# First 256 tokens of a decoder layer turned and multiplied without their norm, the norm's roots applied to five results

## The chip, the cores and the metric

The kernel runs on one core of one Trainium2 chip. The metric is device time in microseconds (us). Each instruction belongs to an engine: PE multiplies matrices, DVE and ACT do elementwise work on tiles, POOL (GpSimd) does a little of that and issues some transfers, and SP issues most transfers. Each engine runs its own instructions in the order in which it gets them.

## The reference

One layer is computed for 512 prompt tokens and 32 sample tokens (8 sequences of 4), with a model width of 1024. What matters here is its beginning:

```python
def _rmsnorm(x, g):
    x32 = x.astype(jnp.float32)
    y = x32 * lax.rsqrt(jnp.mean(x32 * x32, axis=-1, keepdims=True) + EPS) * g.astype(jnp.float32)
    return y.astype(x.dtype)
...
h = _rmsnorm(x, norm_mix_pre)
proj = h @ w_in
xr, q, k, v, g = jnp.split(proj, [c0, c1, c2, c3], axis=-1)
```

The root (the reciprocal root of a token's mean square) is one number for each token, and the gain `g` is one number for each of the 1024 inputs. Behind this stand a convolution and a recurrent unit on `xr`, windowed attention on `q`, `k` and `v`, gates, an output projection, a second norm, a feed-forward part with a convolution, and the states that are handed on.

## The kernel before

Activations are kept turned: model inputs on the 128 partitions, tokens along the free axis. The tokens are cut into two halves (line 26, `HALF`): the first has 256 columns, the second 288 (256 prompt tokens and the 32 sample tokens). The input projection is worked in blocks of 128 output columns. One **result** is one such block for one half: eight input chunks `k`, and for each chunk three multiplications, since every operand is held as a high and a low part: weights high by `hH`, weights high by `hL`, weights low by `hH` (`mmhalf`, lines 313 to 320). So a result is 24 matrix multiplications into one PSUM buffer.

Weights arrive raw (`wload`, line 244; one block is 512 KB), and are split by half blocks called units: ACT writes the high part (`wsplit_hi`, line 264), DVE the low part (`wsplit_lo`, line 279; POOL does it for the first block).

The order of PE, ACT, DVE and POOL is the order in which the program writes their instructions (`manual_schedule`). `step` (line 322) writes one result and then calls `tick` (line 192). A tick writes, in this order: the high splits of weights that are due, the side work that is due (`sides`: generators such as `norm_b`, the attention's units, the parameters), what the last result left in `late` (usually its `done`, which takes the result out of PSUM and splits it), the low splits, and what was put into `last`. Three PSUM buffers hold results (`psm`, line 132), so result n+3 cannot start before the `done` of result n is over. Five more (`psx`) hold turned tiles and small products.

The five first blocks (`FIRST`, line 72; one of k, one of v, three of q) are multiplied for the first half of the tokens, then the same five for the second half; after that both halves of a block follow each other. I number them: results 1 to 5, results 6 to 10, and from 11 on the pairs.

The beginning is written out by hand, lines 341 to 473. The loads go to SP in this order: `x0`, gains, `x1`, weight blocks 0 and 1, `x2`, `x3`, `x4` (the sample tokens), block 2, small tables, blocks 3 and 4. Each `x` tile holds 128 tokens and is loaded as two column halves of 256 KB. PE meanwhile multiplies constants (`dummy`, line 377: `WARM` 12 times, then the turning of the gains, then `KEEP` 11 times). `xsquares` (line 402) sums squares, one half on ACT and one on DVE; `xrstd` and `newton_rstd` (lines 410 and 387) make the roots, with a square root on ACT between steps on DVE. For `x0` and `x1` the four half tiles are multiplied by their roots (`scale0`, line 440), turned on PE (line 460), and multiplied by the gains and split by `hsplit` (line 429: ACT the high part, DVE the low part). Result 1 (`first_mm`, line 449) is interleaved with this by hand.

The second half of the tokens is normed beside results 2 to 5 by `norm_b` (line 495): squares and roots in tick 1, scaling in tick 2, turning in two groups of four chunks in ticks 3 and 4. `keep_a` and `keep_b` (lines 482 and 485) copy the turned and normed tokens to `xn`; `put_away` (line 488) sends them and the reciprocal of the roots to DRAM, so that `x` can be had again for the residual.

Of the kernel before, what the change touches and what calls it, by code (L numbers as in the profile page):

```python
# [17 lines left out]
P = 128  # L18
# [103 lines left out]
def hawk_step(ctx, tc, I, O):  # L122
# [198 lines left out]

    def step(key, X, a, done, target=None, look=2, quick=False):
# [27 lines left out]
    def xload(i):  # L350
        t0, n, src = TOK[i]
        for z in range(2):
# [12 lines left out]
    relx = cp.tile([NBK, NH], F32, name="relx")  # L365
    nc.sync.dma_start(out=relx, in_=I["rel_bias"])
# [4 lines left out]
    wload(3)  # L371
    wload(4)
    pv = keep.tile([P, 96], F32, name="pv")
# [26 lines left out]
    dve.memset(ss, 1.0)  # L400

    def xsquares(i):
        n = TOK[i][1]
        jk, jv = T(f"jk{i}"), T(f"jv{i}")
        act.activation(jk[:n, 0:512], xt[i, 0][:n, 0:512], AF.Square, accum_out=ss[:n, 0, i:i + 1])
        xb = xt[i, 1][:n, 0:512]
        dve.scalar_tensor_tensor(out=jv[:n, 0:512], in0=xb, scalar=1.0, in1=xb, op0=ALU.mult, op1=ALU.mult,
                                 accum_out=ss[:n, 1, i:i + 1])

# [23 lines left out]

    xsquares(0)
    xsquares(1)
    act.copy(pv[:, 0:8], ps0[:, 0:8])
    xrstd(0, 2)
    u0, u1 = wclaim(2)

    def scale0(i, z):  # L440
        dve.tensor_scalar(xt[i, z][:, 0:512], xt[i, z][:, 0:512], ss[:, 1, i:i + 1], None, ALU.mult)
# [10 lines left out]
    ps_ta = []  # L452
    wsplit_lo(*wsplit_hi(u0), eng=pool)
    seq = (0, 2, 1, 3, 4, 6, 5, 7)
    for z, k in enumerate(seq + (None,) * 3):
        if z % 4 == 0 and z < KD:
            for kk in (z // 2, z // 2 + 1):
                ps_ta.append(PX(f"ps_ta{kk}"))
                for q in range(4):
                    pe.transpose(ps_ta[-1][:, q * P:(q + 1) * P], xtile(q % 2, 2 * kk + q // 2), ident)  # L460
        if k is not None:
            hsplit(k, 0, ps_ta[k // 2][:, k % 2 * 256:k % 2 * 256 + 256])
        if z == 1:
            wsplit_lo(*wsplit_hi(u1), eng=pool)
        if z == 2:
            dummy(0)
            dummy(1)
        if 2 <= z < KD + 2:
            first_mm(seq[z - 2], 0, 0, start=z == 2)
        if z >= 3:  # L470
            first_mm(seq[z - 3], 0, 1)
    for k in range(KD):
# [14 lines left out]

    def put_away():
        dve.reciprocal(rms, ss[:, 1, :])
# [5 lines left out]
    def norm_b():  # L495
        last.extend(lambda i=i: xsquares(i) for i in (2, 3, 4))
        last.append(lambda: xrstd(2, 5))
        yield
        last.extend(lambda i=i, e=e: xscale(i, e) for i, e in ((2, "av"), (3, "av"), (4, "vv")))
        last.extend(lambda k=k: keep_a(k) for k in range(4))  # L500
        yield
        for k in range(4, KD):
            keep_a(k)
        for k in range(KD):
            ps = PX(f"ps_tb{k}")
            for i in (2, 3, 4):
                t0, n, _ = TOK[i]
                pe.transpose(ps[:, t0 - 256:t0 - 256 + n], xtile(i, k), ident[:n, :n])
            late.append(lambda k=k, ps=ps: hsplit(k, 1, ps[:, :288]))
            tb.append(ps)  # L510
            if k % 4 == 3:
                late.extend(lambda k=k, ps=tb[k]: keep_b(k, ps) for k in range(k - 3, k + 1))
            if k in (3,):
                yield


    rows_b = cp.tile([64, P], F32, name="rows_b")
# [130 lines left out]

    def split_ps(X, k, a, ps, extra=()):
        n = HALF[a][1] - HALF[a][0]  # L650
        act.activation(X.get(k, a, 0), ps[:, :n], AF.Copy)
        for dst, src in extra:
            act.copy(dst, src)
        sub(X.get(k, a, 1), ps[:, :n], f32(X.get(k, a, 0)))

    def q_done(hd, a, ps):
        if a == 0:
            Q.alloc(hd)
            split_ps(Q, hd, a, ps)
        else:  # L660
            split_ps(Q, hd, a, ps, [(qs[:, :, hd, :], ps[:, 256:288].rearrange("p (b t) -> p b t", b=DB))])
# [10 lines left out]
    def k_done(kv, a, ps):  # L672
        if a == 0:
            K.alloc(kv)
            split_ps(K, kv, a, ps)
        else:
# [19 lines left out]
    def v_done(kv, a, ps):  # L696
# [3 lines left out]
        v = vtmp[kv]  # L700
        act.activation(v[:, lo:hi], ps[:, :hi - lo], AF.Copy)
        if a == 1:
# [1206 lines left out]
```

## Time and profile before

| | |
|---|---|
| median of 3 runs | 997.24 us (997.2 to 997.45) |
| profiled execution, its own time | 998.22 us |
| span of its instructions | 995.9 us, 20166 instructions |
| PE busy | 986.5 us (99%), 7811 instructions |
| DVE busy | 731.6 us (73%) |
| ACT busy | 579.7 us (58%) |
| POOL busy | 167.2 us (17%) |
| moved by DMA | 135.90 MB |

Times inside the trace count from the first instruction of the span; 2.3 us of the profiled execution lie outside it. A timeline row reads: start, length, engine, line, operation, the tiles written and read, the number of instructions merged, and in brackets how long the engine stood idle before and for whom it waited. A matrix multiplication's length includes its passage through the array, so that neighbours overlap: what a stream of them costs is the distance of their starts. "PEld" rows are weight loads beside PE. `SPq` rows are transfers being issued.

### The profile page before, as it was taken

The page shows a single profiled execution, that of the slowest core. Times are in us where ns is not written, and L with a number is a line of the kernel's source. Part 1 is how long each engine was busy: PE and PEld are TensorE (multiplying, and loading weights), DVE is VectorE, ACT ScalarE, POOL GpSimd, SP SyncE. Part 2 cuts the span into 40 slices and gives each one's busy share as a digit, 9 for nine tenths or more (in the row PEclk, how much of TensorE's full clock was granted, in tenths as well). Part 3 has the DMA queues.
Part 4 walks back from the last instruction along what each step waited for, and adds up shares of the span by engine and source line. Part 5 has one row for each costly group of instructions (what it writes and reads, how often), then busy time and mean ns, then how long its engine had stood idle before and what let it go on. Part 6 is the DMA issues. An engine that isn't in the chain of part 4 may idle for free.

```text
span 995.9 us, 20166 instructions
## 1 busy us (share of the span) xinstructions
PE 986.5 (99%) x7811; PEld 976.2 (98%) x7811; DVE 731.6 (73%) x1537; ACT 579.7 (58%) x1417; POOL 167.2 (17%) x277
## 2 busy tenths in 40 slices
PE   9999999999999999999999999999999999999997
PEld 8999999999999999999999999999999999999996
DVE  6477687645936656589787788888888888888765
ACT  6535455469458625456776655555655555556652
POOL 1152010002304473210001010101010101011004
PEclk9999999999999999999999999999999999999999
DMA  7756323333322634236147767676767676768612
GB/s 209 184 142 216 90 71 104 103 86 102 91 84 86 207 92 140 74 106 196 47 117 155 164 151 168 151 167 152 166 152 167 152 167 152 167 145 205 196 45 90
DMA packets 211782, 135.90 MB, mean 136 GB/s; under 512 B 9501, under 2 KB 197677, under 8 KB 211656
## 3 DMA queue, kind: packets, MB, share of 16 engines
q1 hardware_dynamic: 199720, 113.00, 39.8%
q0 software_dynamic: 11920, 19.59, 12.1%
q10 hardware_dynamic: 48, 2.03, 0.8%
q8 instruction: 61, 1.00, 0.4%
q14 instruction: 33, 0.27, 0.1%
HBM read 112.06 MB, written 11.37 MB: 124 GB/s over the span
## 4 chain that ended last, share of the span: by engine, by line
PE 94%; DVE 2%; DMA 1%; ACT 1%; SPq 1%; issue 0%; DVEq 0%; ACTq 0%
PE pmin L163 21%; PE pmdn L163 17%; PE pux L1458 16%; PE puy L1458 8%; PE pq L1458 6%; PE pmout L163 5%; PE pmlo L163 5%; PE pmao L163 5%; PE puz L1458 4%; PE pg L163 1%; PE psc L163 1%; PE pvp L163 1%; PE ptok L163 1%; SPq L354 1%; DMA raw_in<-in_w_in_dram 1%; PE pt L753 1%
## 5 line engine op out<-in xcount | busy, mean ns | idle before, releaser
L163 PE MATMUL pmin<-hH,wh_in 128*128 128x256 f32 (+1 forms) x568 | 165.9, 292 | 0.0
L163 PE MATMUL pmin<-hL,wh_in 128*128 128x256 f32 (+1 forms) x568 | 163.6, 288 | 0.0
L163 PE MATMUL pmin<-hH,wl_in 128*128 128x256 f32 (+1 forms) x568 | 163.3, 287 | 0.3 <-DVE wl_in L280 0.3
L163 PE MATMUL pmdn<-fH,wh_dn 128*128 128x256 f32 (+1 forms) x448 | 129.3, 289 | 0.1
L163 PE MATMUL pmdn<-fH,wl_dn 128*128 128x256 f32 (+1 forms) x448 | 129.2, 288 | 0.0
L163 PE MATMUL pmdn<-fL,wh_dn 128*128 128x256 f32 (+1 forms) x448 | 129.0, 288 | 0.0
L175 DVE SCALAR_TENSOR_TENSOR uc<-u,fv,uc 128x560 f32<-128x560 f32 x128 | 102.0, 797 | 13.3 <-ACT uc L1489 13.2
L163 PEld LDWEIGHTS pmin<-hH,wh_in 128*128 128x128 f32 x568 | 107.0, 188 | 1.5 <-issue 1.2
L163 PEld LDWEIGHTS pmin<-hH,wl_in 128*128 128x128 f32 x568 | 106.8, 188 | 0.5 <-DVE wl_in L280 0.5
L163 PEld LDWEIGHTS pmin<-hL,wh_in 128*128 128x128 f32 x568 | 107.0, 188 | 0.0
L163 PEld LDWEIGHTS pmdn<-fH,wh_dn 128*128 128x128 f32 x448 | 84.4, 188 | 0.5 <-issue 0.5
L163 PEld LDWEIGHTS pmdn<-fL,wh_dn 128*128 128x128 f32 x448 | 84.3, 188 | 0.0
L163 PEld LDWEIGHTS pmdn<-fH,wl_dn 128*128 128x128 f32 x448 | 84.3, 188 | 0.0
L1584 ACT COPY u<-pux 128x272 f32<-128x272 f32 x52 | 20.1, 387 | 84.2 <-PE pux L1458 84.1
L166 DVE TENSOR_TENSOR u<-puy,u 128x240 f32<-128x240 f32 (+2 forms) x78 | 24.6, 344 | 49.5 <-PE puy L1458 32.3
L172 DVE TENSOR_TENSOR ft<-ft,pmdn 128x256 f32<-128x256 f32 (+1 forms) x104 | 45.2, 435 | 17.1 <-PE pmdn L163 16.5
L275 ACT ACTIVATE wh_in<-raw_in 128x512 fp32r<-128x512 f32 x72 | 44.4, 631 | 17.0 <-PE pmin L163 5.8
L1489 ACT ACTIVATE uc<-u,fv 128x560 f32<-128x560 f32 x64 | 48.2, 755 | 0.0
L280 DVE TENSOR_TENSOR wl_in<-raw_in,wh_in 128x512 fp32r<-128x512 f32 x70 | 46.9, 683 | 0.8 <-ACT wh_in L275 0.7
L716 ACT ACTIVATE s<-s,st 128x256 f32<-128x256 f32 (+1 forms) x32 | 15.2, 475 | 50.6 <-DVE st L713 41.4
L1384 POOL DMA_DIRECT2D raw_up_s<-raw_up_s x26 | 22.7, 874 | 99.9 <-DMA raw_up_s<-raw_up__10515 4.5
L166 DVE TENSOR_TENSOR wl_dn<-raw_dn,wh_dn 128x512 fp32r<-128x512 f32 x56 | 38.3, 684 | 0.0
(781 smaller groups left out, 3426.6 us busy)
## 6 DMA issues: line engine op xcount, KB each, us to landing
raw_in<-in_w_in_dram SPq DMA_DIRECT2D x36, 512.0 KB
raw_dn<-in_w_down_dram SPq DMA_DIRECT2D x56, 256.0 KB
raw_up_s<-in_w_up_dram SPq DMA_DIRECT2D x25, 512.0 KB
raw_up_s<-raw_up_s POOLq DMA_DIRECT2D x26, 256.0 KB, 5.8
raw_ao<-in_w_attn_o_dram SPq DMA_DIRECT2D x8, 512.0 KB
raw_lo<-in_w_lru_o_dram SPq DMA_DIRECT2D x8, 512.0 KB
raw_out<-in_w_out_dram SPq DMA_DIRECT2D x8, 512.0 KB
xdram<-xn POOLq DMA_DIRECT2D x8, 272.0 KB, 23.1
```

What stands on the lines that cost most here:

```text
L163: pe.matmul(out, l, r, start=start, stop=stop)
L166: dve.tensor_tensor(out=out, in0=a, in1=b, op=ALU.subtract)
L172: dve.tensor_tensor(out=out, in0=a, in1=b, op=ALU.add)
L175: dve.scalar_tensor_tensor(out=out, in0=a, scalar=s_, in1=b, op0=op0, op1=op1)
L275: act.activation(hl[0], raw, AF.Copy)
L280: (eng or dve).tensor_tensor(out=hl[1], in0=raw, in1=f32(hl[0]), op=ALU.subtract)
L354: nc.sync.dma_start(out=xt[i, z][:n, 0:512], in_=src[:, 512 * z:512 * z + 512])
L716: act.activation(s3[:, j, :], s3[:, j, :], AF.Exp, bias=ng[:, j:j + 1], accum_out=sm[:, j:j + 1])
L1384: pool.dma_start(out=w["p4"], in_=w["p2"], accum_op=ALU.add)
L1458: pe.matmul(ps[:, :HN], w, x, start=start and k == 0 and i == 0, stop=stop and k == 3 and i == 2, skip_group_check=True)
L1489: act.activation(yt[j][:, 0:FLATU], u[:, 0:FLATU], AF.Copy, scale=fv[:, j:j + 1])
L1584: act.copy(e[nm_], z)
```

## The change

The first 256 tokens are no longer multiplied by their roots before they are turned. They are turned as loaded, multiplied by the gains and split, and results 1 to 5 are made from that. As the root belongs to a token, and a token to a column of a result, the results are multiplied by the roots when they are taken out of PSUM (`scaled`: one more multiplication on DVE for k and q into a temporary, which ACT and DVE then split; for v the multiplication takes the place of ACT's copy). For this the roots are spread over all partitions as `r0`: DVE puts them on the diagonals of two 128x128 tiles, PE multiplies these by ones, ACT copies the product. For the blocks from result 11 on, the operand of the first half is remade with the norm, from the kept tokens: for each of the eight chunks DVE multiplies by gain and root, ACT writes the high part, DVE the low part, two chunks in each of four ticks.

The loads are reordered: `x0` and `x1` by column halves, each with the matching half of weight block 0; block 2 between `x2` and `x3`; blocks 3 and 4 ahead of three small loads of other gains; the gains of this norm through ACT. The side work moves: squares and roots of `x2` to `x4` to ticks 2 to 4, the turning of their first four chunks to tick 5, of the last four into the middle of result 6. `done` of results 1 to 5 is written behind the low splits (`last`). The constants' multiplications become 5, 2 and 2. What is kept for the first 256 tokens is unnormed, and the root put away for them is 1.

```diff
+FILL = 2
-WARM = 12
-KEEP = 11
+WARM = 5
+KEEP = 2
...
+        elif between:
+            mmhalf(ps, key, X, a, range(4))
+            between()
+            mmhalf(ps, key, X, a, range(4, 8))
...
-            (last if first_ else late).append(lambda: done(a, ps))
+            (last if len(wunits) <= 2 * FIRST and a == 0 else late).append(lambda: done(a, ps))
...
+    act.dma_start(out=rows_a[0:8, :], in_=I["norm_mix_pre"].rearrange("o (k p) -> (o k) p", p=P))
...
-    xload(0)
-    nc.sync.dma_start(out=rows_a[0:8, :], in_=I["norm_mix_pre"].rearrange("o (k p) -> (o k) p", p=P))
-    xload(1)
-    wload(0)
+    raw0 = wraw[0] = rp.tile([P, KD, P], F32, tag="raw", name="raw_" + wname(0))
+    for z in range(2):
+        xload(0, (z,))
+        xload(1, (z,))
+        nc.sync.dma_start(out=raw0[:, 4 * z:4 * z + 4, :], in_=wsrc(order[0])[:, 4 * z:4 * z + 4, :])
     wload(1)
     xload(2)
+    wload(2)
     xload(3)
     xload(4)
-    wload(2)
...
+    wload(3)
+    wload(4)
...
-    xsquares(0)
-    xsquares(1)
+    xsquare(0, 0, True)
+    xsquare(1, 0, False)
     act.copy(pv[:, 0:8], ps0[:, 0:8])
-    xrstd(0, 2)
     u0, u1 = wclaim(2)
-    scale0(0, 0)
-    scale0(1, 0)
-    act.activation(xt[1, 1][:, 0:512], xt[1, 1][:, 0:512], AF.Copy, scale=ss[:, 1, 1:2])
-    scale0(0, 1)
...
+    for z, u in enumerate((u0, u1)):
+        for kk in (2 * z, 2 * z + 1):
+            ps_ta.append(PX(f"ps_ta{kk}"))
+            for q in range(4):
+                pe.transpose(ps_ta[-1][:, q * P:(q + 1) * P], xtile(q % 2, 2 * kk + q // 2), ident)
+        ks = [4 * z + q for q in (0, 2, 1, 3)]
+        for q, k in enumerate(ks):
+            if q == z:
+                wsplit_lo(*wsplit_hi(u), eng=pool)
+            hsplit(k, 0, ps_ta[k // 2][:, k % 2 * 256:k % 2 * 256 + 256])
+        if z == 0:
+            xsquare(1, 1, False)
+        for q, k in enumerate(ks):
+            first_mm(k, 0, 0, start=z == 0 and q == 0)
+            if q:
+                first_mm(ks[q - 1], 0, 1)
+        first_mm(ks[3], 0, 1)
+        for q in range(FILL if z == 0 else 0):
+            dummy(q)
...
+    def turn_b(ks):
+        for k in ks:
+            ps = PX(f"ps_tb{k}")
+            for i in (2, 3, 4):
+                t0, n, _ = TOK[i]
+                pe.transpose(ps[:, t0 - 256:t0 - 256 + n], xtile(i, k), ident[:n, :n])
+            tb.append(ps)
+        for k in ks:
+            hsplit(k, 1, tb[k][:, :288])
+
+    def norms():
+        dg = T("dg_0")[:, 0:256]
+        last.append(lambda: xsquare(0, 1, True))
+        last.append(lambda: xrstd(0, 2))
+        last.extend(lambda i=i: dve.tensor_scalar(dg[:, i * P:(i + 1) * P], ident, ss[:, 1, i:i + 1], None, ALU.mult)
+                    for i in range(2))
+        yield
+        ps = PX("ps_r0")
+        mm(ps[:, 0:256], ones, dg, True, True)
+        act.copy(r0, ps[:, 0:256])
+        last.append(lambda: xsquares(2))
+        yield
+        last.extend(lambda i=i: xsquares(i) for i in (3, 4))
+        yield
+        last.append(lambda: xrstd(2, 5))
+        last.extend(lambda k=k: keep_a(k) for k in range(4))
+        last.extend(lambda i=i, e=e: xscale(i, e) for i, e in ((2, "av"), (3, "av"), (4, "vv")))
+        last.extend(lambda k=k: keep_a(k) for k in (4, 5))
+        yield
+        turn_b(range(4))
+        keep_a(6)
+        keep_a(7)
+        for k in range(4):
+            keep_b(k, tb[k])
+        yield
+        for k in range(KD):
+            t = T(f"rn{k}")[:, 0:256]
+            stt(t, xn[k][:, 0:256], pv[:, G_PRE + k:G_PRE + k + 1], r0, ALU.mult, ALU.mult)
+            act.activation(h.get(k, 0, 0), t, AF.Copy)
+            sub(h.get(k, 0, 1), t, f32(h.get(k, 0, 0)))
+            if k % 2:
+                yield
+
+    def turn_more():
+        turn_b(range(4, KD))
+        for k in range(4, KD):
+            keep_b(k, tb[k])
...
+    def scaled(ps):
+        t = T("ev")[:, 0:256]
+        mul(t, ps[:, 0:256], r0)
+        return t
+
-    def split_ps(X, k, a, ps, extra=()):
+    def split_ps(X, k, a, ps, extra=(), raw=False):
         n = HALF[a][1] - HALF[a][0]
+        if raw:
+            ps = scaled(ps)
...
-    start_at(1, norm_b())
+    start_at(1, norms())
     start_at(13, put_away())
-    start_at(2, attn_tables())
+    start_at(3, attn_tables())
...
-        step(("in", c), h, 1, in_done(c), target=2 * FIRST + (0, 2, 4, 6, 6)[z])
+        step(("in", c), h, 1, in_done(c), target=2 * FIRST + (0, 2, 4, 6, 6)[z],
+             between=turn_more if z == 0 else None)
```

More of the change, by code (lines that the diff above doesn't have):

```diff
@@ L320, in mmhalf, with step @@
             mm(ps[:, :n], wl, xh, False, k == KD - 1)
-    def step(key, X, a, done, target=None, look=2, quick=False):
+    def step(key, X, a, done, target=None, look=2, quick=False, between=None):
         first_ = key == order[0] and a == 0
@@ L348, in hawk_step, with xload @@
     xt = {}
[L350 removed]
+    def xload(i, halves=(0, 1)):
         t0, n, src = TOK[i]
[L352 removed]
+        for z in halves:
             xt[i, z] = S(f"x{i}_{z}")
             nc.sync.dma_start(out=xt[i, z][:n, 0:512], in_=src[:, 512 * z:512 * z + 512])
[L356 to L359 removed]
+    raw0 = wraw[0] = rp.tile([P, KD, P], F32, tag="raw", name="raw_" + wname(0))
[3 more added lines that the diff above has]
+        nc.sync.dma_start(out=raw0[:, 4 * z:4 * z + 4, :], in_=wsrc(order[0])[:, 4 * z:4 * z + 4, :])
     wload(1)
     xload(2)
+    wload(2)
     xload(3)
     xload(4)
[L364 removed]
     relx = cp.tile([NBK, NH], F32, name="relx")
@@ L400, in hawk_step, with xsquare @@
     dve.memset(ss, 1.0)
-    def xsquares(i):
[L403 to L408, printed above, removed]
+    def xsquare(i, z, on_act):
+        n = TOK[i][1]
+        j_, x_, o_ = T(f"jk{i}_{z}")[:n, 0:512], xt[i, z][:n, 0:512], ss[:n, z, i:i + 1]
+        if on_act:
+            act.activation(j_, x_, AF.Square, accum_out=o_)
+        else:
+            dve.scalar_tensor_tensor(out=j_, in0=x_, scalar=1.0, in1=x_, op0=ALU.mult, op1=ALU.mult, accum_out=o_)
+    def xsquares(i):
+        xsquare(i, 0, True)
+        xsquare(i, 1, False)
     def xrstd(lo, hi):
@@ L452, in hawk_step @@
     ps_ta = []
[L453 to L461, printed above, removed]
-            hsplit(k, 0, ps_ta[k // 2][:, k % 2 * 256:k % 2 * 256 + 256])
[L463 to L471, printed above, removed]
+    for z, u in enumerate((u0, u1)):
[7 more added lines that the diff above has]
+                wsplit_lo(*wsplit_hi(u), eng=pool)
+            hsplit(k, 0, ps_ta[k // 2][:, k % 2 * 256:k % 2 * 256 + 256])
+        if z == 0:
[7 more added lines that the diff above has]
+            dummy(q)
     for k in range(KD):
@@ L493, in put_away @@
             yield
[L495 to L504, printed above, removed]
+    r0 = S("r0")[:, 0:256]
+    def turn_b(ks):
+        for k in ks:
             ps = PX(f"ps_tb{k}")
@@ L700, in v_done @@
         v = vtmp[kv]
-        act.activation(v[:, lo:hi], ps[:, :hi - lo], AF.Copy)
+        if a == 0 and 18 + kv in qkv_order[:FIRST]:
+            mul(v[:, lo:hi], ps[:, :hi - lo], r0)
+        else:
+            act.activation(v[:, lo:hi], ps[:, :hi - lo], AF.Copy)
         if a == 1:
```

13 lines of the change are left out of this document (3 added, 10 removed).

## The prediction

> **What bounds the kernel now.** I read the page first, then PE's waits over the whole span, then three windows behind the head, cut at result 2 (16.92), result 6 (33.72) and result 11 (53.05).
>
> ```profile
> PE 986.5 (99%) x7811; PEld 976.2 (98%) x7811; DVE 731.6 (73%) x1537; ACT 579.7 (58%) x1417; POOL 167.2 (17%) x277
> ```
> ```profile
> PE ps_warm L163 <- POOL epst L216: 1.5, 1, 1.5
> PE pst_f L163 <- DVE accx L172: 0.4, 1, 0.4
> PE ps_ta L460 <- DVE x L441: 0.4, 1, 0.4
> PE pmdn L163 <- ACT ffn_rows_s L1675: 0.4, 1, 0.4
> PE pmin L163 <- DVE wl_in L280: 0.3, 1, 0.3
> ```
> ```profile
> 16.92:33.72 16.80, 16.55 (x124) 14.32 (x123) 14.31 (x39) 14.03 (x37) 1.86 (x2) 1.00 0.64 153
> 33.72:53.05 19.33, 19.33 (x152) 18.85 (x150) 7.74 (x22) 8.63 (x23) 1.88 (x2) 1.00 0.63 174
> 53.05:63.56 10.51, 10.51 (x89) 10.51 (x88) 7.14 (x25) 4.42 (x20) 7.75 (x35) 1.00 0.55 163
> ```
>
> In a window row stand its stretch, its length and then, each with a count, the busy time of PE, PEld, DVE, ACT and POOL. PE waits 3 us of 996. From result 2 on it is the bound, so whatever moves PE's work at 60 us moves the end by as much, and there are two questions: how much earlier result 1 ends, and whether DVE and ACT then keep up. The windows warn for the second: while results 2 to 5 run DVE is already busy 14.31 of 16.80 us and ACT 14.03.
>
> ```profile
> 1.52 5.49 PE L163 MATMUL ps_warm<-ident,ones 128*128 128x128 f32 x24 [1.52 <-POOL epst L216]
> ...
> 5.76 0.63 ACT L405 ACTIVATE jk<-x 128x512 f32<-128x512 f32 x1 [1.56 <-DMA x<-in_x_prompt_dram]
> ...
> 7.09 2.72 PE L163 MATMUL ps_warm<-ident,ones 128*128 128x128 f32 x22
> ...
> 7.54 0.69 DVE L407 SCALAR_TENSOR_TENSOR jv<-x 128x512 f32<-128x512 f32 x1 [2.70 <-DMA x<-in_x_prompt_dram]
> ...
> 8.35 0.16 DVE L172 TENSOR_TENSOR ss<-ss 128x2 f32<-128x2 f32 x1
> ...
> 9.66 1.28 DVE L441 TENSOR_SCALAR x<-x,ss 128x512 f32<-128x512 f32 x3
> ...
> 10.20 1.38 PE L460 MATMUL ps_ta<-ident,x 128*128 128x128 f32 x8 [0.39 <-DVE x L441]
> ...
> 10.86 0.31 SPq L366 DMA_DIRECT2D relx<-in_rel_bias_dram  x1
> ...
> 12.51 1.56 ACT L431 ACTIVATE hH<-ps_ta,pv 128x256 fp32r<-128x256 f32 x4
> 12.51 1.04 PE L460 MATMUL ps_ta<-ident,x 128*128 128x128 f32 x8
> 12.69 1.28 POOL L280 TENSOR_TENSOR wl_in<-raw_in,wh_in 128x512 fp32r<-128x512 f32 x1 [0.43 <-ACT wh_in L275]
> ...
> 15.98 1.11 PE L163 MATMUL pm_first<-hH,wl_in 128*128 128x256 f32 x8
> ```
> ```profile
> SPq L366 <- DMA raw_in<-in_w_in_dram: 0.7, 1, 0.7
> ```
>
> The head is a chain: the last `x` half lands (7.54), squares, roots (8.35 to 9.66), scaling, turning (10.20), splits, products; result 2 follows at 16.92.
>
> **Result 1 under the change.** Landings: the third 256 KB tile came at 5.76, the fourth by 7.54, weight block 1 at about 10.86 (a transfer queued behind it waited for that). Block 0 lies between; I take 9.2, the middle. The new order brings the same bytes, so by place in the queue: first half of block 0 about 5.8, second half of `x` about 8.4, second half of block 0 about 9.2.
>
> PE starts slow: 24 passes in 5.49 us are 0.229 each, the 22 from 7.09 on 0.124 with their tail, 0.11 without. Five constants (ten passes) end at 3.8, the gains and two more constants at 4.9, eight turnings at twice their 0.11 at 6.65. ACT splits weights at 5.8 (0.52) and four chunks (1.56 for four, 0.37 apart) to about 8.0, DVE behind it; the first eight products end near 8.8, two constants at 9.1. Second half: turning to 10.0; ACT chunk 4 at 10.0, weights 10.35 to 10.9, chunks 6, 5, 7 to 12.0; DVE's last low part at 12.7; the eight low-weight products (0.118 apart in the row at 15.98) to 13.9; POOL's low split, 10.9 and 1.28, is out by 12.2. **Result 2 starts at 13.9 instead of 16.92: 3.0 us gained.** PE's fillers and ACT's order set this, and moving the three landings by 1 us either way hardly changes it.
>
> **Results 2 to 6.** These are the prices, from rows of the same operations:
>
> ```profile
> 19.35 1.13 ACT L275 ACTIVATE wh_in<-raw_in 128x512 fp32r<-128x512 f32 x2
> ...
> 20.16 1.29 DVE L280 TENSOR_TENSOR wl_in<-raw_in,wh_in 128x512 fp32r<-128x512 f32 x2
> ...
> 20.39 0.36 ACT L651 ACTIVATE kH<-pm_first 128x256 fp32r<-128x256 f32 x1
> ...
> 21.38 0.42 DVE L166 TENSOR_TENSOR kL<-pm_first,kH 128x256 fp32r<-128x256 f32 x1
> ```
> ```profile
> L175 DVE SCALAR_TENSOR_TENSOR hL<-ps_ta,pv,hH x8: 473/476/485, 11.8 to 15.2; 128x256 fp32r<-128x256 f32 x8
> ```
> ```profile
> 20.66 1.32 ACT L421 ACTIVATE x<-x,ss 128x512 f32<-128x512 f32 x2
> 21.89 1.17 ACT L483 COPY xn<-ps_ta 128x256 f32<-128x256 f32 x4
> ```
> ```profile
> 23.61 2.18 PE L508 MATMUL ps_tb<-ident,x 128*128 128x128 f32 x12
> ```
>
> The product that spreads the roots is new on PE: 256 columns in the constants' two passes are about 0.46. The roots' chain leaves DVE by 15.6 and hides under result 2 (13.9 to 16.7). `r0` is there at 17.65, result 3 starts at 17.2 and result 4 at 20.2.
>
> From 17.65 DVE works without a pause (neighbours overlap by some 0.08 each): k scaled, split by ACT, lowered (0.42 + 0.36 + 0.42 = 1.2), squares 0.6, a wait for ACT 0.2, low splits 1.2, v 0.35, two squares 1.2, a table copy 0.25, low splits 1.2, q 1.2, and the roots of `x2` to `x4`, which before took 9.66 - 8.35 = 1.3. That ends at 26.35. Result 5 ends at 26.1; before, PE went into line 508 at 23.61 without a wait. Now it waits: ACT makes the four copies (1.17) from 25.5 and then scales two tiles (1.32) to 27.9. PE turns from 27.3, needs 2.18 and another gap of 0.6, and is through at 30.1: **1.8 us lost.** The other half of the turning now lies inside result 6.
>
> ```profile
> 45.77 0.29 PE L163 MATMUL pmin<-hH,wl_in 128*128 128x288 f32 x1
> ...
> 46.95 0.30 PE L163 MATMUL pmin<-hH,wl_in 128*128 128x288 f32 x1
> ```
>
> Nine products of 288 columns lie between these two, 0.131 each, so 24 are 3.15. Result 7 starts at 30.1 + 3.15 + 2.1 = 35.4; before it was 33.72 + 3.15 = 36.9. The lead is 1.5.
>
> **Results 7 to 14: the remade operand.** The windows say that DVE has room from 33.72 to 53.05 (7.74 of 19.33), but what comes is a chain through two engines that both work in order: multiply 0.476, ACT 0.36, subtract 0.42, then the next chunk; some 1.25 a chunk (hand-offs and overlap cancel), **10.0 us for eight**, though only 6.5 are busy time. What is queued behind it on DVE are the `done`s that free PSUM for PE, and the low splits.
>
> ```profile
> 47.21 0.42 DVE L175 SCALAR_TENSOR_TENSOR s<-psc,btab 128x256 f32<-128x256 f32 x1 [5.72 <-DMA btab<-rrep]
> ...
> 49.90 0.46 DVE L166 TENSOR_TENSOR qL<-pmin,qH 128x288 fp32r<-128x288 f32 x1 [1.34 <-ACT qs L653]
> ...
> 54.08 0.45 DVE L166 TENSOR_TENSOR qL<-pmin,qH 128x288 fp32r<-128x288 f32 x1
> ```
> ```profile
> 53.05 0.28 PE L163 MATMUL pmin<-hH,wh_in 128*128 128x256 f32 x1
> ```
> ```profile
> 56.03 0.38 PE L163 MATMUL pmin<-hH,wh_in 128*128 128x288 f32 x1
> ```
> ```profile
> 63.20 0.61 PE L753 MATMUL pt<-ident,s 128*128 128x128 f32 x4
> 63.56 0.38 PE L163 MATMUL pmin<-hH,wh_in 128*128 128x288 f32 x1
> ```
>
> From 29.0 DVE lowers four chunks (2.0, at the pace of the turning), copies two (0.75), does q of result 4 (1.2), four chunks (1.75), two copies (0.75): 35.5. Two chunks 2.45, q of result 5 1.2: 39.2, and only then may result 8 begin, which PE could have begun at 38.6. Two chunks 2.45, k 0.65, low splits 1.2; two chunks 2.45, low splits 1.2; two chunks 2.45: 49.55. The attention's first unit, which stood at 47.21 behind its table, starts here; up to the end of result 8's `done` it takes 49.90 + 0.46 - 47.21 = 3.15, so 52.7 against 50.36 before. Result 11, needing that buffer, starts at 52.8 against 53.05. Low splits 1.2, parameters and attention 2.6 (54.08 less the 1.2 and 0.37 behind 49.90), `done` of result 9 0.45: 56.95: result 12 starts at 57.0 against 56.03. From there PE is the bound again, and DVE's `done` has over 2 us to spare by result 14 (the old order had 3). Result 14 would start 63.56 - 56.03 = 7.5 later, at 64.5. The same adding-up applied to the old order from 16.92 on gives 52.9, 55.8 and 63.2 where the trace has 53.05, 56.03 and 63.56. Taken against itself, the change costs 64.5 - 63.2 = **1.3 us**.
>
> The profiled execution took 998.22 us (995.9 of span and 2.3 around it); it would become 999.5. The median of the runs is 1.0 lower, 997.24, so I predict **998.5**. About 0.2% (2 us) is what a measurement of this kernel can tell from no change.
>
> **Bounds of what the trace does not show.** The remade chunk works from SBUF, its nearest rows from PSUM. If the new DVE work is 20% shorter, result 14 comes 1.4 earlier (-0.1 in all); if 25% longer, 1.9 later (+3.2). Without any of the chain the sum is -1.1. The landings I bounded by rows and their effect is under 0.5. Two pieces of 512 KB took from 7.54 to 10.86, so `x2` and block 2 land near 14.2; ACT reaches block 2 at 14.3, and 0.8 us of lateness would hide behind the roots' chain on DVE, more would show in result 3. Blocks 3 and 4 are reached only at 19.0 and 21.3, two pieces later each; they now pass nothing but small gain rows, which nobody needs before tick 9. The gains' transfer on ACT lies before ACT's first input.
>
> **The clock at the start.**
>
> ```profile
> PEclk9999999999999999999999999999999999999999
> ```
>
> In the head's rows PE ran at half pace until about 7, though it had worked without a gap since 1.5 and the page shows the granted clock as full. So it quickens only after a stretch of unbroken work. The change takes work away there: constants until 4.9, then turnings, then products that wait for ACT. If turnings count as work, PE at half pace has hardly a gap until 9 and quickens at 7 or 8; I take that. If they do not, unbroken work begins only with result 1's last products near 12, and the pace doubles around 16: the head's end and most of result 2 run at half pace, +2.4 us to the sum, 3.7 in all.
>
> The Trainium skill (TensorE: Matmul & The Clock Gate, Part 1) says that the array stays at half rate until a free-running window of about 3.4 us was busy, and Part 4 there says that a transpose does not count as busy in the same way; by that rule the change would come out slower. The trace agrees on the half pace; no row of it shows what turnings count for.
>
> **The rivals.**
> - *The gain survives.* If the remaking hides in DVE's idle 11.6 us of the second window, the lead of 1.5 at result 7 stays, 995.7; if PE's wait at 27 goes too, -3.0 + 0.46, 994.7. It decides from a remade chunk of about 0.9 us downwards. For it: that window row. Against it: 10 us of chain, and the buffers behind it.
> - *PE stays slow* (the clock above): 1001. It decides if the quickening comes after 10.
> - *DVE's lag is longer than I added up*: the buffers' wait continues past result 12 and takes 25% more for each new piece, 1000.5 to 1001.
> - *The halves bring nothing*: if the second halves land 2 us later than I say, the head starts later by 1 to 2 us and everything behind it too: 999.5 to 1000.5, within the third.
>
> **How the numbers follow.** My forecast, a small loss, 997.0 to 1000.0: 0.50. The gain survives (994.5 to 997.0): 0.24, of which 0.10 is below 995.25. Slow clock: 0.13. Longer lag: 0.13. Of the first case 0.14 lies above 999.23. So faster by over 0.2%: 0.10; slower: 0.14 + 0.13 + 0.13 = 0.40; same: 0.50. The range leaves out the best part of the second case and the worst of the last two: 995.0 to 1001.5; the forecast's own is 997.0 to 1000.0.
>
> **What would show it.** Right: result 2 near 14; a wait of PE for scaled tokens of 1 to 2 us near 27; waits of `pmin` for PSUM, freed by DVE, at 39, 53 and 57; DVE without long idle time from 17 to 60. Wrong: result 2 at 16 or later, with passes of 0.2 us in it (the clock); no PE wait behind result 6 (the gain survives); DVE's remade chunks far from 1.25 apart.

## The result and the profile after

| | before | changed |
|---|---|---|
| median of 7 runs | 997.45 us (996.94 to 998.37) | 1000.54 us (999.47 to 1002.82) |
| ratio | | 1.0034, 95% interval 1.0021 to 1.0046 |
| profiled execution, span | 998.22 us, 995.9 us | 1000.54 us, 998.8 us |
| result 2, result 12, result 14 start | 16.92, 56.03, 63.56 | 14.79, 60.23, 67.76 |

The change costs 3.1 us. The forecast was 998.5, a loss of 1.3 us; the time lies above the forecast's own range (997.0 to 1000.0) and inside the full one. The direction and the two places of the loss were foreseen, its size was not.

The engines' line of the changed kernel, and PE's waits over its whole span (engine, tile, line, who released it: us in all, times, longest):

```profile
PE 985.0 (99%) x7781; PEld 972.8 (97%) x7781; DVE 740.5 (74%) x1558; ACT 581.9 (58%) x1424; POOL 167.2 (17%) x277
```
```profile
PE pmin L164 <- DVE qL L167: 2.1, 2, 1.3
...
PE ps_tb L505 <- ACT x L432: 1.4, 2, 1.1
```

PE's busy time is 1.5 us below that of before (985.0 against 986.5, with 30 instructions fewer), and the span is still 2.9 us longer. The two rows are the two waits that the prediction announced: for DVE's taking-out of results, and for the scaled tokens.

The same three windows as before (stretch, length, busy time and count of PE, PEld, DVE, ACT, POOL, then PEclk, DMA share, GB/s), and below them PE's busy time and PEclk in windows of 2 us:

```profile
16.92:33.72 16.80, 15.37 (x108) 13.76 (x107) 13.60 (x35) 11.79 (x31) 1.93 (x2) 0.93 0.58 130
33.72:53.05 19.33, 19.25 (x139) 17.50 (x139) 13.49 (x31) 11.01 (x28) 1.87 (x2) 0.97 0.54 159
53.05:63.56 10.51, 8.40 (x65) 7.96 (x65) 7.34 (x25) 4.59 (x19) 4.60 (x20) 1.00 0.58 177
```
```profile
28.00:30.00 2.00, 1.31 (x6) 1.00 0.62 166
30.00:32.00 2.00, 2.00 (x12) 0.86 1.17 323
32.00:34.00 2.00, 2.00 (x10) 0.50 1.28 172
34.00:36.00 2.00, 2.00 (x12) 0.79 1.16 334
```

One of these windows in the kernel before:

```profile
32.00:34.00 2.00, 2.00 (x20) 1.00 1.24 213
```

PE's busy time in the first window fell from 16.55 to 15.37 and in the third from 10.51 to 8.40: the waits. The column that nobody expected is PEclk, 1.00 in every such window of before up to 70 us. Near 31.4, behind the wait for tokens and the turnings that follow it, the granted clock falls to a half, and it comes back near 35. What was not granted is 0.14, 0.50 and 0.21 of 2 us each, 1.7 us of PE's work; at half clock that is a stretch of 3.4 us. PE counts as fully busy all the while, so no table of busy shares or waits shows this loss.

The timeline of the same place (start, length, engine, line, operation, tiles, count, and in brackets the idle time before and its releaser):

```profile
26.99 0.28 PE L164 MATMUL pmin<-hH,wl_in 128*128 128x256 f32 x1
28.41 0.33 PE L505 MATMUL ps_tb<-ident,x 128*128 128x128 f32 x1 [1.15 <-ACT x L432]
29.02 2.15 PE L505 MATMUL ps_tb<-ident,x 128*128 128x128 f32 x11 [0.28 <-ACT x L432]
31.10 0.40 PE L164 MATMUL pmin<-hH,wh_in 128*128 128x288 f32 x1
...
31.49 0.44 PE L164 MATMUL pmin<-hH,wl_in 128*128 128x288 f32 x1
31.73 0.44 PE L164 MATMUL pmin<-hH,wh_in 128*128 128x288 f32 x1
...
38.06 0.29 PE L164 MATMUL pmin<-hH,wh_in 128*128 128x288 f32 x1
```

Result 5's last product starts at 26.99, the turning at 28.41 instead of 27.1, and from 31.49 on the products of 288 columns are 0.24 apart instead of 0.131. Result 7 starts in the last row, at 38.06; before it was 36.9. The lead of 2.1 us that the head had given is gone before the remaking has begun.

The remaking, on DVE:

```profile
38.18 0.48 DVE L176 SCALAR_TENSOR_TENSOR rn<-xn,pv,r 128x256 f32<-128x256 f32 x1
39.14 0.42 DVE L167 TENSOR_TENSOR hL<-rn,hH 128x256 fp32r<-128x256 f32 x1 [0.48 <-ACT hH L538]
39.48 0.48 DVE L176 SCALAR_TENSOR_TENSOR rn<-xn,pv,r 128x256 f32<-128x256 f32 x1
...
59.73 0.45 DVE L167 TENSOR_TENSOR qL<-pmin,qH 128x288 fp32r<-128x288 f32 x1
```
```profile
56.07 0.39 PE L164 MATMUL pmin<-hH,wh_in 128*128 128x256 f32 x1 [1.27 <-DVE qL L167]
...
60.23 0.40 PE L164 MATMUL pmin<-hH,wh_in 128*128 128x288 f32 x1 [0.85 <-DVE qL L167]
...
67.76 0.38 PE L164 MATMUL pmin<-hH,wh_in 128*128 128x288 f32 x1
```

A chunk is 1.30 us behind the one before it, and in each DVE stands 0.48 waiting for ACT to write the high part. Results 11 and 12 then wait for the `done`s that stand behind this chain. From result 12 on PE is the bound again: result 14 follows 7.53 later, as before, and is 4.2 us later than before. The medians differ by only 3.1. The spans differ by 2.9, because the profiled execution of before ran a little slow further on, where both kernels do the same: from 600 to 900 us its window counts 2388 products on a PE without a gap, that of the changed kernel 2397, nine more, or 1.1 us at 0.126 each. The times of the two profiled executions differ by 2.3, because 1.7 us lie outside the span of the changed kernel and 2.3 outside that of before; it is much the same in every later run (1.7 to 2.0 against 2.2 to 2.5), and none shows why. And the profiled execution of before was 0.8 us above its median of 7.

### The profile page after: what moved, and what is told of

Same layout as the page of the kernel before. It is cut to its first block, busy times and chain, and to the rows that moved or that the text cites. A ratio compares the mean times of both kernels' runs of the same rounds, so it can differ in the third digit from the quotient of the medians.

```text
span 998.8 us, 20141 instructions
## 1 busy us (share of the span) xinstructions
PE 985.0 (99%) x7781; PEld 972.8 (97%) x7781; DVE 740.5 (74%) x1558; ACT 581.9 (58%) x1424; POOL 167.2 (17%) x277
## 4 chain that ended last, share of the span: by engine, by line
PE 86%; DVE 6%; ACT 4%; DMA 2%; issue 1%; SPq 1%; DVEq 0%; ACTq 0%
PE pmin L164 19%; PE pmdn L164 17%; PE pux L1500 16%; PE puy L1500 8%; PE pmout L164 5%; PE pmao L164 5%; PE pmlo L164 5%; PE puz L1500 4%; PE pq L1500 2%; DVE uc L176 1%; DMA raw_in<-in_w_in_dram 1%; PE pg L164 1%; PE pvp L164 1%; PE psc L164 1%; PE ptok L164 1%
```

## The experiments

The theory after this comparison: there are three losses, each the result of an order. PE waits for scaled tokens, because their roots stand on DVE behind other work; this idle time costs PE its clock, 1.7 us beside the 1.4 of the wait; and the remaking holds DVE in a chain through two engines. The rivals: the turnings and not the waiting cost the clock (the rule on transposes that the prediction quotes from the Trainium skill); or DVE simply has too much work between 17 and 60 us, in whatever order.

Every ratio below is to the kernel before in runs on the same chip (medians of before there: 998.1 to 998.3 us), with its 95% interval.

**PE kept busy over the wait.**

```diff
     def turn_b(ks, fill=0):
         for k in ks:
             ps = PX(f"ps_tb{k}")
+            for z in range(fill if k == ks[0] else 0):
+                mm(ps[:, (z % 4) * P:(z % 4 + 1) * P], ones, ident, True, True)
...
-        turn_b(range(4))
+        turn_b(range(4), fill=6)
```

> The changed kernel, with six multiplications of constants put on PE in front of the first turning of the second half's tokens, so that PE works while it waits near 27.3 to 28.4. Nothing else is changed, and the wait itself is not shortened. Theory (idle PE loses its clock, and the slow stretch is worth 1.7 us): the granted clock stays 1.00 from 31 to 35, where it was 0.50 at 32 to 34; the first half of result 6 takes 1.6 us instead of 2.79; result 7 starts near 36.4 instead of 37.97, the DVE's chain of remade chunks 1.6 earlier, and the time falls from 1000.5 to 998.9, with less spread between runs. Rival 1 (turnings alone cost the clock, since 2.7 us of them still follow): 0.50 is seen again and the time stays 1000.5. Rival 2 (DVE's order, not PE, sets results 11 and 12): the clock is back, but result 14 still starts near 67.5 and the time is 1000 to 1000.5.

Measured: 999.47 us, ratio 1.0010 (1.0001 to 1.0019) where the changed kernel has 1.0034 and later 1.0033: about 2.3 us less for six multiplications that compute nothing.

```profile
30.00:32.00 2.00, 2.00 (x11) 1.00 1.24 279
32.00:34.00 2.00, 2.00 (x15) 1.00 1.18 225
```

The clock stays. Result 14 starts at 67.22 instead of 67.76, which looks like a gain of only 0.5; but in this execution the clock was lost earlier, in the head:

```profile
10.00:12.00 2.00, 2.00 (x12) 0.50 1.12 337
12.00:14.00 2.00, 1.68 (x7) 0.72 1.12 334
```

and result 2 started at 15.72, 0.93 later than in the changed kernel's profile. From result 2 to result 14 it took 51.50 us against 52.97: 1.5 us less, near the 1.6 expected. Rival 1 fails for this case, since 2 us of turnings still follow. Rival 2 fails too, although 67.22 is near the 67.5 that it named: counted from result 2, the chain on DVE begins 21.9 us later instead of 23.4, and the time is below its 1000.

**The remaking in pairs, by kind of step.** The same instructions: two multiplications, then two high parts on ACT, then two low parts.

```diff
-        for k in range(KD):
-            t = T(f"rn{k}")[:, 0:256]
-            stt(t, xn[k][:, 0:256], pv[:, G_PRE + k:G_PRE + k + 1], r0, ALU.mult, ALU.mult)
-            act.activation(h.get(k, 0, 0), t, AF.Copy)
-            sub(h.get(k, 0, 1), t, f32(h.get(k, 0, 0)))
-            if k % 2:
-                yield
+        for k in range(0, KD, 2):
+            t = [T(f"rn{k + j}")[:, 0:256] for j in range(2)]
+            for j in range(2):
+                stt(t[j], xn[k + j][:, 0:256], pv[:, G_PRE + k + j:G_PRE + k + j + 1], r0, ALU.mult, ALU.mult)
+            for j in range(2):
+                act.activation(h.get(k + j, 0, 0), t[j], AF.Copy)
+            for j in range(2):
+                sub(h.get(k + j, 0, 1), t[j], f32(h.get(k + j, 0, 0)))
+            yield
```

> The changed kernel, with the two remade chunks of a tick written by kind of step: both multiplications on DVE, both high parts on ACT, both low parts on DVE. The same instructions, another order. Theory (the remade operand costs a chain through two engines): a pair takes 1.9 us of DVE instead of 2.6, all four 2.8 us less, the waits of results 11 and 12 for DVE (1.27 and 0.85) go, and the time falls by their 2.1 to 998.4. The wait at 27 and the half clock near 32 stay. Rival (the waits come from the attention's unit and its table load on ACT, or from DVE's sheer amount of work): the pairs get shorter but results 11 and 12 still wait more than 1.5 together, and the time is 1000 to 1000.5.

Measured: 997.28 us, ratio 0.9988 (0.9979 to 0.9997), some 4.6 us below the changed kernel and more than the 2.1 expected. DVE in the same place:

```profile
38.57 0.87 DVE L176 SCALAR_TENSOR_TENSOR rn<-xn,pv,r 128x256 f32<-128x256 f32 x2
39.53 0.82 DVE L167 TENSOR_TENSOR hL<-rn,hH 128x256 fp32r<-128x256 f32 x2
40.27 0.42 DVE L170 TENSOR_TENSOR ev<-pmin,r 128x256 f32<-128x256 f32 x1
```

A pair takes 1.70 (38.57 to 40.27) instead of 2.60, without a stop for ACT, and no wait of results 11 or 12 is left. Result 10 starts as in the changed kernel (50.63 against 50.65) and result 12 at 57.59 instead of 60.23: 2.64 gained where the two recorded waits were 2.12. A wait costs PE more than its idle time says, because that counts from the modelled end of a product, 0.28 behind its start, while products follow each other at 0.12. The rest of the 4.6 is not settled: the two medians come from two chips, the intervals are about 1 us wide on each side, and how often the clock is lost differs from run to run (below).

**The roots earlier.** Squares of `x2` on ACT, whose queue was empty there; the roots finished ahead of the taking-out of result 3; first column halves scaled first; the copies of the first tokens ahead of them.

```diff
+        xsquare(2, 0, True)
+        xsquare(2, 1, True)
         act.copy(r0, ps[:, 0:256])
-        last.append(lambda: xsquares(2))
+        last.append(lambda: xsquares(3))
         yield
-        last.extend(lambda i=i: xsquares(i) for i in (3, 4))
+        last.append(lambda: xsquares(4))
+        last.append(lambda: rstd_a(2, 5))
         yield
-        last.append(lambda: xrstd(2, 5))
-        last.extend(lambda k=k: keep_a(k) for k in range(4))
-        last.extend(lambda i=i, e=e: xscale(i, e) for i, e in ((2, "av"), (3, "av"), (4, "vv")))
+        last.insert(0, lambda: rstd_b(2, 5))
+        last.insert(1, lambda: xscale1(4, 0, "v"))
+        for k in range(4):
+            keep_a(k)
+        last.insert(2, lambda: xscale1(2, 0, "a"))
+        last.insert(3, lambda: xscale1(3, 0, "a"))
         last.extend(lambda k=k: keep_a(k) for k in (4, 5))
+        last.append(lambda: xscale1(4, 1, "v"))
         yield
         turn_b(range(4))
+        xscale1(2, 1, "a")
+        xscale1(3, 1, "a")
```

(`rstd_a` and `rstd_b` are the sum with the square root, and the rest of `xrstd`; `xscale1` scales one column half.)

> The changed kernel, with the roots of x2 to x4 and the scaling of their first column halves moved ahead of the taking-out of result 3, the squares of x2 both on ACT before the roots are spread, the copies of the first tokens ahead of the scaling, and the second column halves scaled later. The remade operand is as in the changed kernel. Theory (the wait at 27 is DVE's order, and it brings the clock loss with it): PE turns at 27.3 without a wait, the clock stays 1.00, result 6 starts near 29.4 and result 7 near 34.8 instead of 37.97; the chain of remade chunks starts 2.4 earlier, so the waits at results 8, 11 and 12 together are no smaller than before and the time falls by about 2.4 to 998.1. Rival 1 (turnings cost the clock by themselves): half pace in result 6 in spite of no wait, 999.8. Rival 2 (the remade chain ends where it ended, whatever comes before): 1000.5.

Measured: 998.23 us, ratio 1.0005 (0.9996 to 1.0014), about 2.8 us below the changed kernel. PE's longest wait between 3 and 80 us, and the turning:

```profile
PE pmin L164 <- DVE qL L167: 2.1, 2, 1.3
```
```profile
27.37 2.18 PE L527 MATMUL ps_tb<-ident,x 128*128 128x128 f32 x12
29.48 0.40 PE L164 MATMUL pmin<-hH,wh_in 128*128 128x288 f32 x1
```

The wait for tokens and, with it, the half clock are gone (PEclk 1.00 in every window from 28 to 38). The waits for DVE are the same 2.1 as before: everything, the chain too, is earlier by the same amount, 2.55 at result 14 (65.21). Both rivals fail. The edit is not one of order alone: one square and two scalings, some 1.8 us, went from DVE to ACT, and what this did for the wait at 27 and what the order did was not tried apart.

**Both, with the pairs behind the taking-out of results.** Early roots, and the pairs put into `last` of their tick.

> The edit of the early roots, and the remade chunks in pairs written by kind of step and put behind the taking-out of the results and the low splits of their tick. Theory (order is the whole of the loss; DVE has time enough): no wait at 27, none at results 8, 11 and 12, full clock; result 7 near 34.8, result 11 near 51.0 against 53.05 in the kernel before, so 2 us faster than the kernel before: 995.4. Rival (DVE's amount of work is the bound from 17 to 57): results 11 and 12 still wait, 997 to 998.5.

Measured: 997.36 us, ratio 0.9994 (0.9985 to 1.0003): 2 us short of what was expected and inside the 997 to 998.5 of the rival. One wait of a microsecond is left, result 12's:

```profile
PE pmin L164 <- DVE qL L167: 1.0, 1, 1.0
```
```profile
49.86 0.46 DVE L167 TENSOR_TENSOR qL<-pmin,qH 128x288 fp32r<-128x288 f32 x1 [2.02 <-ACT qs L727]
...
51.43 0.88 DVE L176 SCALAR_TENSOR_TENSOR rn<-xn,pv,r 128x256 f32<-128x256 f32 x2
...
55.74 0.45 DVE L167 TENSOR_TENSOR qL<-pmin,qH 128x288 fp32r<-128x288 f32 x1
```

Putting the pairs behind had been my own idea, and it failed by its place: DVE stands 2.02 idle ahead of 49.86, and then the last pair comes in the way of the next `done` (55.74).

**The same with the pairs left in front**, beside the changed kernel itself on one chip.

> The changed kernel once more, beside the others of this call on one chip, so that they can be set against it and not only against the kernel before. Expected by every theory: 1.0034 of the kernel before (1.002 to 1.0046), the wait of 1.4 us near 28, half clock near 32 to 34, and waits of results 11 and 12 for DVE of 2.1 us together.

> The edit of the early roots and the remade chunks in pairs by kind of step, but left where the changed kernel has them, ahead of the taking-out of the results. Theory (three losses: the wait, the clock and the chain; the wait of result 12 that remained when the pairs stood behind the taking-out came from that place alone): no wait of PE from result 6 on, full clock, result 7 near 35.5, result 11 near 51.7, result 12 near 54.7, result 14 near 62.3 against 63.56 in the kernel before; 0.998 of the kernel before, some 4.5 to 5 us faster than the changed kernel. Rival (DVE's amount of work is the bound): results 8, 11 or 12 wait by 1 us or more, and the time is that of the kernel before, 0.9995 to 1.0005.

The changed kernel again: 1001.24 us, ratio 1.0033 (1.0021 to 1.0045). With early roots and pairs: 995.40 us, ratio 0.9973 (0.9964 to 0.9982), 5.8 us below it and faster than the kernel before. PE's waits between 3 and 80 us, and the start of result 14:

```profile
PE pm_first L164 <- ACT wh_in L276: 0.6, 1, 0.6
PE pm_first L164 <- ACT hH L464: 0.5, 1, 0.5
PE pmin L164 <- DVE wl_in L281: 0.2, 1, 0.2
```
```profile
61.89 0.38 PE L164 MATMUL pmin<-hH,wh_in 128*128 128x288 f32 x1
```

Result 14 is 1.7 us ahead of the kernel before. The rival of DVE's amount of work fails: the pairs by themselves ended the waits of results 11 and 12 with the same instructions on the same engines, and here the whole loss is gone although DVE was relieved of no more than 1.8 us.

**Without the remaking** (the loop leaves the operand as it is).

> The kernel with early roots and pairs, without the remaking: results 11 and later use the unnormed operand for the first 256 tokens, so this part of the computation is left out. Theory (in pairs the remaking is hidden): within 0.3 us of the kernel with the remaking. Rival (it still delays the taking-out of results, or the reads of the attention's table): 1 us or more faster.

Measured: 995.65 us, ratio 0.9976 (0.9967 to 0.9984), result 14 at 61.84 against 61.89. In pairs the remaking costs nothing that these runs could show. DVE's rows in the window from 33.72 to 53.05, with it and then without:

```profile
33.72:53.05 19.33, 19.33 (x151) 18.85 (x152) 16.82 (x45) 12.34 (x35) 1.95 (x3) 1.00 0.64 180
```
```profile
33.72:53.05 19.33, 19.33 (x151) 18.85 (x152) 12.62 (x34) 9.36 (x26) 3.90 (x7) 1.00 0.73 196
```

PE is busy for all 19.33 us in both, with DVE at 16.82 or at 12.62: 4.2 us less work on DVE bring nothing.

**Turnings and the clock.** Each of the twelve turnings ahead of result 6 done twice, then four times, into the same place, on the kernel with early roots and pairs.

```diff
-                pe.transpose(ps[:, t0 - 256:t0 - 256 + n], xtile(i, k), ident[:n, :n])
+                for _ in range(4 if k < 4 else 1):
+                    pe.transpose(ps[:, t0 - 256:t0 - 256 + n], xtile(i, k), ident[:n, :n])
```

> The kernel with early roots and pairs, in which each of the twelve turnings ahead of result 6 is done twice into the same place; nothing but PE's time there is added. PE then turns for 4.3 us without a wait and without an ordinary multiplication, where the changed kernel had 3.8 us made of 1.4 us idle and 2.4 us of turnings. Theory A (idle time takes the clock, turnings keep it): granted clock 1.00 throughout, result 6 starts 2.1 to 2.2 later than with single turnings and the whole is 2 us longer than that kernel. Theory B (a turning does not count as work for the clock): half pace in result 6 and a granted clock of 0.50 near 32 to 35, another 1.7 us, 3.8 in all, less what DVE's slack hides.

> The kernel with early roots and pairs, with each of the twelve turnings ahead of result 6 done four times into the same place. A repeated turning took 0.109 us where the doubled ones were tried, so PE now turns for some 5.6 us (27.3 to 33) with neither a wait nor an ordinary multiplication, well beyond the 3.8 us of waiting and turning after which the changed kernel lost its clock. Theory A (idle time takes the clock, turnings keep it): granted clock 1.00, result 6 starts near 33.0 and its products of 288 columns are 0.131 apart. Theory B (a turning is no work for the clock): granted clock 0.50 somewhere in 31 to 37, turnings or products 0.21 to 0.24 apart.

Twice: 995.95 us, ratio 0.9981 (0.9971 to 0.9990), full clock. Twelve turnings take 2.11 us (27.37 to 29.48 above) and 24 took 3.25, so a repeated one cost only 0.095, less than the 0.109 written down for the next run, and the stretch decided nothing. Four times: 997.89 us, ratio 1.0002 (0.9993 to 1.0011):

```profile
27.11 5.56 PE L528 MATMUL ps_tb<-ident,x 128*128 128x128 f32 x48
...
32.84 0.29 PE L164 MATMUL pmin<-hL,wh_in 128*128 128x288 f32 x1
32.97 0.29 PE L164 MATMUL pmin<-hH,wl_in 128*128 128x288 f32 x1
```
```profile
30.00:34.00 4.00, 4.00 (x34) 1.00 1.20 255
34.00:38.00 4.00, 4.00 (x25) 1.00 0.27 82
```

5.5 us of turnings and nothing else, and from the second on the products behind them are 0.13 apart. Theory B fails: turnings by themselves keep the clock. Where the Trainium skill (TensorE: Matmul & The Clock Gate, Part 4) says that a transpose does not count as busy in the same way, these turnings differ, and the measurement decides. The table under "Why this matters for your kernels" on that page of the Trainium skill advises against idle gaps of over about 3 us; here gaps of 1.15 and 0.28 us in a stretch of 4 us went with a loss.

That the waiting takes the clock is only half shown. All three profiles with the full wait for tokens lost it, and none of the nine that have 0.3 us of it or none; by their mean granted clock of 0.999, though, two of the eleven runs with pairs alone (995.25 and 995.35) may have kept it in spite of the wait. But the waits of results 11 and 12, 1.27 and 0.85 us among products, left it at 1.00 in the same profile of the changed kernel:

```profile
54.00:56.00 2.00, 0.80 (x7) 1.00 0.37 82
56.00:58.00 2.00, 1.93 (x16) 1.00 0.33 111
```

It was so in all four profiles that have these two waits. So a wait of over a microsecond is not enough by itself, and here it was wait and turnings together that went with the loss. The turnings behind the wait are 0.18 apart (2.11 us for 12), those of the run with four 0.11 (5.49 for 48): whether such sparse turnings count as idle in part, or the 1.43 us of idle time are just over a bound that 1.27 is not, was not tried.

**The clock in the head.** The changed kernel's second profile had lost the clock twice:

```profile
12.00:14.00 2.00, 1.77 (x8) 0.57 1.10 348
...
30.00:32.00 2.00, 2.00 (x9) 0.70 1.19 274
32.00:34.00 2.00, 2.00 (x9) 0.50 1.11 231
34.00:36.00 2.00, 2.00 (x10) 0.50 1.06 308
36.00:38.00 2.00, 2.00 (x10) 0.59 0.16 60
```

By the same sum as above, with 0.58 from 10 to 12, 1.7 us of PE's work was not granted in the head and 3.4 behind the wait, twice 1.7. The waits do not decide this alone either: PE waited 0.73 and 0.76 us ahead of the two losses in the head, and 0.71 and 0.90 in the same place of two profiles that kept the clock. So constants were put where PE waits in the head:

```diff
                 pe.transpose(ps_ta[-1][:, q * P:(q + 1) * P], xtile(q % 2, 2 * kk + q // 2), ident)
+        for q in range(2 + z):
+            dummy(q)
```

> The kernel with early roots and pairs, with two multiplications of constants behind the first group of turnings and three behind the second, where PE waits 0.35 to 0.7 us for the first split chunks. Theory (the short waits in the head cost the clock in some executions, as between 8 and 14 us in two of the profiles so far, 0.9 us each time at result 2): the clock is 1.00 from 8 to 14 in every profile, result 2 stays near 14.5 to 14.8, the spread of the runs falls and the median falls by 0 to 0.5 us against the same kernel without them (0.9973 of the kernel before): 0.997. Rival (the clock in the head is lost whatever PE does there, or the constants stand in the way): the same spread, and the same time or up to 0.5 slower.

> The kernel with early roots and pairs once more, beside the filled head on one chip: 0.9973 of the kernel before (0.9964 to 0.9982) by every theory.

With the head filled: 994.49 us (994.39 to 994.65, 5 runs), ratio 0.9965 (0.9952 to 0.9977). The same kernel without: 995.74 us (994.40 to 996.58, 11 runs), ratio 0.9972 (0.9963 to 0.9981). The gain is larger than expected and the spread falls from 2.2 us to 0.3. Between 3 and 80 us one wait of PE is left, 0.2 us for DVE.

The lowest time without the filling (994.40) is the usual one with it. That fits a clock lost in some runs and not in others, and so does the mean granted clock of each run: 0.998 to 1.000 in all five filled runs and in the four fastest unfilled ones (994.40 to 994.77), 0.996 to 0.998 in the seven others (995.71 to 996.58). A loss of 1.7 in 993 us would be 0.0017 of it. Where in the slower runs the clock was lost is argued, not shown: the one profile of the unfilled kernel on that chip is of a fast run and kept its clock from 8 to 16.

## Why the prediction was partly right

- **Result 2 at 13.9, 3.0 us gained: the mechanism was right, the size not.** It came at 14.79, 2.1 us ahead. The first half of block 0 was the late term: ACT split it at 6.38 instead of 5.8, PE was through with the first products and constants at 10.03 instead of 9.1, and the fifth chunk began on ACT at 10.67 instead of 10.0. So the sentence that moving the landings by 1 us hardly changes the sum did not hold: ACT stood idle for this one until 6.38, and its lateness was passed on.

```profile
6.38 0.63 ACT L276 ACTIVATE wh_in<-raw_in 128x512 fp32r<-128x512 f32 x1 [1.96 <-DMA raw_in<-in_w_in_dram]
...
10.67 0.47 ACT L442 ACTIVATE hH<-ps_ta,pv 128x256 fp32r<-128x256 f32 x1 [1.88 <-PE ps_ta L459]
```
```profile
10.03 1.04 PE L459 MATMUL ps_ta<-ident,x 128*128 128x128 f32 x8
```

- **The clock at the start: the choice was right, as far as it went.** Eight turnings at full pace at 10.03 (1.04 us; the eight from 5.16 took 1.91) show that PE had become quick by 10, so the rival of a slow head, which quickens after 10, is refuted. But the clock was weighed only for the start.
- **"1.8 us lost" at 27: right.** Result 5 ended at 27.1 (26.1 foreseen, the head's lateness), the turning, worth 2.18, was through at 31.10 (30.1 foreseen): 1.8 lost.
- **"Result 7 starts at 30.1 + 3.15 + 2.1 = 35.4" is the step that failed.** It came at 38.06, 2.7 later: 1.0 from the turning's end, and 1.7 because the sum puts the products behind a wait at full pace. Both experiments that took away the idle time, by constants or by earlier roots, brought the clock back.
- **The remaking, "some 1.25 a chunk": right.** Results 11 and 12 waited as foreseen; at result 8 no wait was left, since PE itself was late by then. A chunk took 1.30; ACT's copy took 0.42, not 0.36. The chain began 2.7 late (38.18 for 35.5) and so result 12 came 3.2 late (60.23 for 57.0): the error of the clock was carried through, and half a microsecond was added.
- **The add-up of 64.5 for result 14** became 67.76, 3.3 more: 1.0 of the head and the wait, 1.7 of the clock, 0.6 of the chain's pace and of the waits' hidden part. Set against the kernel before, result 14 lost 4.2 where the forecast had 1.3, and yet the time missed by 2.0 and not by 2.9. That is luck: about 0.5 of it the changed kernel saves outside its span, which the sum did not know of, and the rest is no more than runs differ by.
- **The rivals.** That the gain survives needed a remade chunk of 0.9 us or less; in pairs it is 0.85, and then the kernel is indeed faster than before. As the change is written the condition fails. "DVE's lag is longer" gave 1000.5 to 1001, which is the measured time, but by pieces 25% longer; the pieces were 0.48 and 0.42 as priced. The number was right for the wrong reason. The second halves' landings played no part: ACT took the second half of block 0 at 11.04, straight behind the fifth chunk, without a wait for its transfer.

## What to carry to other kernels

A wait of PE is priced by its idle time, by the pipeline's latency, and by the clock behind it: look at PEclk in windows of 2 us after every wait of a microsecond, since busy shares hide it and not every such wait costs it, and fill the wait with work that computes nothing if it cannot be removed. Where one engine's output goes through another and back, write such pieces by kind of step, two at a time: here that made 10 us of chain cost nothing without one instruction fewer. And when an operation is deferred to save a head, place what it defers by asking which result's taking-out is queued behind it.

## What the runs showed of the hardware

- Idle gaps of 1.15 and 0.28 us within 4 us, with turnings between and behind them, went with half the clock for 3.4 us in two profiles and for twice that in a third; the windows give 1.7 us of ungranted work, or 3.4. Gaps of 1.27 and 0.85 us among products left the granted clock at 1.00 in four profiles.
- In the head the clock was lost in two of the eleven profiles of kernels with the unfilled head: result 2 came at 15.66 and 15.72 there, at 14.36 to 15.14 in the nine others.
- 5.5 us of turnings alone kept the granted clock at 1.00, and a turning repeated on the same tile took 0.095 us (12 more turnings, 1.14 us more).
- Two recorded waits of 2.12 us cost 2.64 us.
